# Four-layer diffusion-transformer kernel on one core: modulation rows moved between VectorE and TensorE, two convolution tiles in one PSUM bank

## The chip, the cores and the metric

The kernel runs on one core of a Trainium2 chip. The metric is the device time of one execution in microseconds (us), lower is better. The core's engines are named as in the profile: PE is TensorE's matmul and PEld its weight load, DVE is VectorE, ACT is ScalarE, POOL is GpSimd, SP is SyncE, which here issues nearly all DMAs.

## The reference, cut to what matters

The model has four layers of width 2048 over 256 tokens, with 256 context tokens that the kernel carries through layers 0 and 1. Layers 0 and 3 mix with a Fourier transform, layer 1 with window attention, layer 2 with a depthwise convolution (31 taps, one weight per channel and tap) followed by a layer norm. Each layer is modulated: a row vector of 3 x 2048 numbers (shift, scale, gate) comes from `silu(c) @ ada_w[i]`.

```python
def ada_modulation(cond, w, b):
    m = jax.nn.silu(cond) @ w + b
    return jnp.split(m, 3, axis=-1)
...
def conformer_conv_mix(h, w_in, dw_w, dw_b, ln_g, ln_b, w_out):
    a, a_gate, z = jnp.split(h @ w_in, 3, axis=-1)
    g = a * jax.nn.sigmoid(a_gate)
    ...
    y = jax.nn.silu(layer_norm(y, ln_g, ln_b))
    return (y * jax.nn.silu(z)) @ w_out
...
        shift, scale, gate = ada_modulation(c, ada_w[i], ada_b[i])
        h = rms_norm(x, norm_g[i]) * (1.0 + scale[:, None, :]) + shift[:, None, :]
        ...
        x = x + gate[:, None, :] * o
```

All inputs are float32. The kernel keeps float32 accuracy by splitting each operand in a high and a low part and adding up three products (two for the output projections).

## The kernel before, in words

**Weight pieces.** A weight matrix is streamed in pieces of 128 partitions x 1024 columns (`w_piece`, L143). Each piece has a DMA into `raw` (issued by SP, L153 or L155), a CAST on ACT to `whi` (L179), a subtraction `wlo = raw - whi` in two halves on VectorE or in one on GpSimd (L180), and its matmuls: `gemm_T` (L193 to L195) and `gemm_N` (L213 to L215) for the input projections, L1114 and L1115 for the output projections. There are three raw buffers and, up to out_proj(1), two of whi and wlo, from layer 2 on three of each (`wB`, L1181): there a piece takes the buffers of the third piece before it.

**Stages from layer 1 on.** Attention's z columns (`accz`, 32 pieces, L1075); the output projection of layer 1, written out_proj(1) below (`out_proj`, L1093, 32 pieces, accumulators `acco`); layer 2's a and gate columns in eight column groups of eight pieces (`accg`, L1217), each followed by two channel tiles `kt` of the convolution; layer 2's z columns in four groups (`accz`, L1296) with the layer norm fed in between (`ln_part`, L1260); out_proj(2); layer 3; its out_proj(3). An output projection adds to the residual on VectorE (L1126), sums squares (L416), and its last two column groups also prepare the next layer's input (L482).

**Modulation steps.** A group is one third of a layer's modulation and takes 16 steps; a step is 128 rows of ada_w times one entry of silu(c) per partition. Its 128 x 2048 block comes by two DMAs of 512 KB each into two of the four `aw` buffers (L326). On VectorE a step is two multiply-adds of 128 x 1024 into `adacc` (L279 for the first of a group, L281 else), called halves below; on TensorE it is four matmuls of 512 columns (L268), the first step of a TensorE chain with a stationary operand padded to 32 columns (`cpad`, L264). At a group's end VectorE's sums are added over partitions by four matmuls (L295), and the result goes to `modc`. The stream `ada_v` has seven groups, for (layer, third) = (1,2), (2,0) to (2,2), (3,0) to (3,2).

**The plan.** `Stream.plan(quarters, steps)` (L350) sets a goal of 4 x quarters steps in all and spreads what is missing over the coming calls of `step`, one behind each weight piece. The goals are the constants T1 to T3S: T1 in attention (56 calls), T1O in out_proj(1) (SV1 = 28 calls), T2 in accg from group 2 on, on TensorE (46 calls), T2Z in z, T2O in out_proj(2) (SV2 = 22 calls), then `nxt3` (until group (3,1) is done, T3S), then plan(28, 60) in layer 3. `ada_v.behind` (L283, L540) keeps the first half of a stage behind the start of a layer.

**The convolution.** GpSimd writes the gated tile into `gp` (L1241), ACT the first tap into PSUM with the bias (L1244), VectorE the 30 others in place (L1250), ACT copies the result out to `cv` (L1252), and the channel sums go to `csum` (GpSimd, the last on VectorE, L1258). The tile `pv` has the size of a PSUM bank and only its first half is used; there are two such buffers (tag "cv"). The taps' weights come by two DMAs (`dwr`, L1174) in `nxt2`, called at the start of out_proj(1)'s seventh column group; TensorE turns them (L1201) in layer 2.

**The order.** The Tile scheduler orders each engine's instructions statically by dependencies, buffers and priorities, so the plan's numbers and the buffers decide what stands where; an engine executes its row in order.

Of the kernel before, what the change touches and what calls it, by code (L numbers as in the profile page):

```python
# [19 lines left out]
P = 128  # L20
# [3 lines left out]
TAPS = 31  # L24
# [4 lines left out]
T0O = 9  # L29
T1 = 14.25  # L30
T1O = 18.25
T2 = 21
T2Z = 21
T2O = 24
T3S = 24.5
SA = 22
# [35 lines left out]
def dit_kernel(ctx: ExitStack, tc: tile.TileContext, x, c, ctxt, c_ctx, norm_g, ada_w, ada_b,  # L72
# [32 lines left out]
    nc.vector.memset(eps_t[:], EPS)  # L105
    sel = cp.tile([P, 2], F32, name="sel")
    for o in range(2):
        nc.vector.tensor_reduce(sel[:, o:o + 1], ident[:, o:o + 97:32], axis=AX.X, op=ALU.add)

    sel8 = cp.tile([P, 8], F32, name="sel8")  # L110
# [141 lines left out]
    def ada_group(l, s, st):  # L252
# [3 lines left out]
        for kt in range(KT):  # L256
            aw = st.get(l, s, kt)
            if st.pe:
# [4 lines left out]
                if fp:  # L263
                    cs = wp.tile([P, 40], F32, tag="cpad", name="cpad")[:, :32]  # L264
                    nc.vector.memset(cs, 0.0)
                    nc.vector.tensor_copy(cs[:, 0:2], csil[:, kt, :])
# [200 lines left out]
    class Deferred:  # L467
# [3 lines left out]
        def __init__(self, l):  # L471
            self.l, self.rs, self.done = l, None, 0
            t = wp.tile([P, 40], F32, tag="cpad", name=nm("sh"))
            self.sh, self.col = t[:, 0:2 * KT].rearrange("p (k r) -> p k r", r=2), t[:, 32:36]
            sv = modc[l][:, 0:16, 0]
            nc.scalar.copy(self.sh[:, :, 0].bitcast(F32R), sv)
            nc.vector.tensor_sub(self.sh[:, :, 1], sv, self.sh[:, :, 0])
# [40 lines left out]
        def leave(self, dst, bank, func, i):  # L518

            col = self.col[:, i:i + 1]  # L520
            nc.scalar.copy(col, bank[:, 256:257])
# [145 lines left out]
    csil0 = aw0.tile([P, 4, 32], F32, name="csil0")  # L667
    nc.gpsimd.memset(csil0[:], 0.0)
    psD = pool(l0, "psD0", PSUM)
    psa_box[0] = pool(l0, "psada0", PSUM)  # L670
# [500 lines left out]
    def nxt2():  # L1171
        for i in range(2):
            t = wp.tile([P, D // 2], F32, tag="aw", bufs=AWB, name=nm("dwr"))
            nc.sync.dma_start(t[:TAPS, :], conv_dw_w[0, :, i * 1024:(i + 1) * 1024])  # L1174
            dwr.append(t)
        return Deferred(2)
# [40 lines left out]
    for cg in range(8):  # L1217
# [20 lines left out]
        for ci in range(2):  # L1238
            kt = 2 * cg + ci
            gt = gp[kt % 4]  # L1240
            nc.gpsimd.tensor_mul(gt[:, PAD:PAD + 256], sa[:, 256 * ci:256 * ci + 256], sg[:, 256 * ci:256 * ci + 256])  # L1241
            pv = psD.tile([P, 512], F32, tag="cv", bufs=2, name=nm("pv"))
            if T0A:
                nc.scalar.activation(pv[:, :256], gt[:, 0:256], AF.Identity, bias=colT[:, kt:kt + 1],  # L1244
                                     scale=dwT[:, kt, 0:1])
            else:
                nc.vector.tensor_scalar(pv[:, :256], gt[:, 0:256], dwT[:, kt, 0:1], colT[:, kt:kt + 1],
                                    op0=ALU.mult, op1=ALU.add)
            for t in range(1, TAPS):
                nc.vector.scalar_tensor_tensor(pv[:, :256], gt[:, t:t + 256], dwT[:, kt, t:t + 1], pv[:, :256],  # L1250
                                               op0=ALU.mult, op1=ALU.add)
            nc.scalar.copy(cv[kt][:], pv[:, :256])  # L1252
            if kt == 0:
                nc.vector.tensor_copy(csum[:], pv[:, :256])
            elif CSP > kt:
                nc.gpsimd.tensor_add(csum[:], cv[kt][:], csum[:])
            else:
                nc.vector.tensor_add(csum[:], pv[:, :256], csum[:])  # L1258

# [64 lines left out]
    yh = [hp.tile([P, 2, 256], F32R, tag=f"yh{k}", name=f"yh3_{k}") for k in range(KT)]  # L1324
    ada_v.plan(28, 60)
    rbox[0] = wk
# [16 lines left out]
    for cg in range(4):  # L1343
        def piece_z(kt):
            return w_piece(w_rows(wi, kt, D + cg * 512), deint=True)

        if cg:
# [111 lines left out]
```

## Time and profile before

| | us |
|---|---|
| median of 3 runs | 1924.52 (1924.08 to 1924.67) |
| the profiled execution's own time | 1923.44 |
| its span | 1921.4 |
| TensorE busy in the span | 1859.0 |
| VectorE busy | 1452.4 |
| ScalarE busy | 911.0 |
| GpSimd busy | 224.5 |

The profile is of one execution; 1923.44 us is its device time, 1921.4 us the span from the first to the last recorded instruction. Instructions are grouped by source line; "busy" is the time in which at least one of a group ran, "mean" the duration of one, "idle before" the time its engine waited just ahead of them, with what ended the wait. A row of the windows view gives, for a stretch from A to B in us, its length, then busy time and instruction count of PE, PEld, DVE, ACT and POOL, then the granted TensorE clock, the busy share of the 16 DMA engines and the GB/s moved. By the chain of starts on PE the stages run as follows: attention's z from 966.6, out_proj(1) from 1093.0 to 1194.4, accg to 1394.9, z to 1494.5, out_proj(2) from 1494.6 to 1598.9, then layer 3. TensorE matmuls leave two records each in the counts.

### The profile page before, as it was taken

Reading aid. Unit: us, or ns where it says so; the run is one execution under the profiler, and the core shown is the slowest. Engines: PE = TensorE matmul, PEld = TensorE weight load, DVE = VectorE, ACT = ScalarE, POOL = GpSimd, SP = SyncE. Lnnn points to the kernel's source line nnn. Section 1 sums busy time; section 2 is a strip of 40 time slices with the busy share of each in tenths; the row PEclk is TensorE's granted clock in tenths of the full one; section 3 lists DMA queues with packets and bytes.
Section 4 is the critical chain, followed back from the end, with each engine's and each line's share of the span. In section 5 each row is a group of like instructions: output and inputs, shape, how many; then the busy total and the mean of one; then the engine's idle time right before and its main releaser. Section 6 shows DMA issues by size and latency. Waiting matters only on the chain.

```text
span 1921.4 us, 30258 instructions
## 1 busy us (share of the span) xinstructions
PE 1859.0 (97%) x11143; PEld 1497.9 (78%) x11143; DVE 1452.4 (76%) x2774; ACT 911.0 (47%) x1685; POOL 224.5 (12%) x124
## 2 busy tenths in 40 slices
PE   6999999999999999999999989999999899999997
PEld 5566657777776687866689978999999788889886
DVE  4899954556653458987898678688898999997675
ACT  6333342233322225455556545644455657656553
POOL 0000000000000000000000000788893000000000
PEclk9999999999999999999999999999999999999999
DMA  8888867666778754741568677577766697785553
GB/s 262 282 292 298 302 241 262 201 233 214 240 240 266 272 192 145 245 161 56 187 197 258 206 246 250 187 247 247 256 211 196 213 308 238 244 284 177 165 175 132
DMA packets 247173, 433.64 MB, mean 226 GB/s; under 512 B 16212, under 2 KB 135732, under 8 KB 247026
## 3 DMA queue, kind: packets, MB, share of 16 engines
q1 hardware_dynamic: 245728, 430.25, 68.3%
q8 instruction: 87, 1.43, 0.3%
q10 hardware_dynamic: 1298, 1.48, 0.3%
q14 instruction: 60, 0.49, 0.1%
HBM read 429.56 MB, written 2.10 MB: 225 GB/s over the span
## 4 chain that ended last, share of the span: by engine, by line
PE 78%; DVE 8%; DMA 7%; ACT 3%; issue 2%; POOL 2%; SPq 0%; ACTq 0%; DVEq 0%; POOLq 0%
PE acco L1114 7%; PE accz L193 5%; PE accz L194 5%; PE accz L195 5%; PE accu L213 4%; PE accu L214 4%; PE accu L215 4%; PE acco L1115 3%; DVE wlo L180 3%; PE pa L268 3%; PE acco L193 3%; PE acco L194 3%; PE acco L195 3%; PE accg L193 3%; PE accg L195 3%; PE accg L194 3%
## 5 line engine op out<-in xcount | busy, mean ns | idle before, releaser
L179 ACT CAST whi<-raw 128x512 fp32r<-128x512 f32 (+1 forms) x765 | 540.9, 761 | 664.0 <-PE accu L215 121.3
L180 DVE TENSOR_TENSOR wlo<-raw,whi 128x512 fp32r<-128x512 f32 x682 | 497.3, 778 | 214.7 <-ACT whi L179 209.4
L281 DVE SCALAR_TENSOR_TENSOR adacc<-aw,csil,adacc 128x1024 f32<-128x1024 f32 x188 | 242.7, 1297 | 74.8 <-DMA aw<-in_ada_w_dram 74.7
L1114 PE MATMUL acco<-yh,whi 128*128 128x512 f32 x768 | 276.1, 403 | 9.5 <-ACT whi L179 4.8
L195 PE MATMUL accz<-hx,wlo 128*128 128x256 f32 (+1 forms) x768 | 220.0, 287 | 6.8 <-DVE wlo L180 5.6
L1115 PE MATMUL acco<-yh,wlo 128*128 128x256 f32 x768 | 217.2, 285 | 2.8 <-DVE wlo L180 2.8
L193 PE MATMUL accz<-hx,whi 128*128 128x256 f32 (+1 forms) x768 | 218.0, 284 | 0.0
L194 PE MATMUL accz<-hx,whi 128*128 128x256 f32 x768 | 217.9, 284 | 0.0
L1250 DVE SCALAR_TENSOR_TENSOR pv<-gp,dwT,pv 128x256 f32<-128x256 f32 x480 | 193.0, 485 | 18.9 <-ACT pv L1244 18.3
L180 POOL TENSOR_TENSOR wlo<-raw,whi 128x1024 fp32r<-128x1024 f32 x83 | 201.7, 2441 | 40.3 <-ACT whi L179 37.6
L1114 PEld LDWEIGHTS acco<-yh,whi 128*128 128x128 f32 x768 | 146.1, 191 | 46.6 <-ACT whi L179 5.4
L195 PEld LDWEIGHTS accz<-hx,wlo 128*128 128x128 f32 x768 | 146.7, 191 | 10.3 <-DVE wlo L180 7.3
L1115 PEld LDWEIGHTS acco<-yh,wlo 128*128 128x128 f32 x768 | 146.9, 192 | 7.0 <-DVE wlo L180 5.7
L194 PEld LDWEIGHTS accz<-hx,whi 128*128 128x128 f32 x768 | 146.6, 191 | 1.2 <-issue 0.8
L193 PEld LDWEIGHTS accz<-hx,whi 128*128 128x128 f32 x768 | 146.9, 191 | 0.6 <-ACT whi L179 0.2
L193 PE MATMUL accg<-hx,whi 128*128 128x256 f32 (+1 forms) x512 | 144.9, 284 | 0.3 <-ACT hx L455 0.3
L195 PE MATMUL accg<-hx,wlo 128*128 128x256 f32 (+1 forms) x512 | 143.9, 282 | 0.0
L194 PE MATMUL accg<-hx,whi 128*128 128x256 f32 x512 | 143.3, 280 | 0.0
L1193 POOL MEMSET gp<- 128x286 f32 x4 | 1.2, 338 | 1193.3 <-PE acco L1115 1193.3
L193 PE MATMUL acco<-yh,whi 128*128 128x512 f32 (+1 forms) x272 | 105.9, 390 | 0.0
L193 PEld LDWEIGHTS accg<-hx,whi 128*128 128x128 f32 x512 | 96.2, 188 | 10.8 <-issue 10.3
L194 PE MATMUL acco<-yl,whi 128*128 128x512 f32 (+1 forms) x272 | 103.6, 381 | 0.0
(283 smaller groups left out, 3713.2 us busy)
## 6 DMA issues: line engine op xcount, KB each, us to landing
aw<-in_ada_w_dram SPq DMA_DIRECT2D x376, 512.0 KB, 5.3
raw<-in_four_w_in_dram SPq DMA_DIRECT2D x126, 512.0 KB, 4.9
raw<-in_attn_w_in_dram SPq DMA_DIRECT2D x72, 512.0 KB, 4.0
raw<-in_conv_w_in_dram SPq DMA_DIRECT2D x128, 256.0 KB, 3.4
raw<-in_four_w_out_dram SPq DMA_DIRECT2D x32, 512.0 KB, 5.8
raw<-in_attn_w_out_dram SPq DMA_DIRECT2D x64, 256.0 KB, 4.7
raw<-in_conv_w_in_dram SPq DMA_DIRECT2D x32, 512.0 KB, 4.3
raw<-in_conv_w_out_dram SPq DMA_DIRECT2D x64, 256.0 KB, 4.2
```

The source lines that it names most:

```text
L179: nc.scalar.copy(hv[:, c], iv[:, c])
L180: eng.tensor_sub(lv[:, c], iv[:, c], hv[:, c].bitcast(F32))
L193: mm(o, a, hh, start=st, stop=False, skip_group_check=True)
L194: mm(o[:, :narrow] if narrow else o, a, hl, start=False, stop=False, skip_group_check=True)
L195: mm(o, b, hh, start=False, stop=kt + k == span[1] - 1, skip_group_check=True)
L213: mm(acc[:], hh, whi[:, k, :], start=st, stop=False)
L214: mm(acc[:], hh, wlo[:, k, :], start=False, stop=False)
L215: mm(acc[:], hl, whi[:, k, :], start=False, stop=kt + k == KT - 1)
L281: ins = nc.vector.scalar_tensor_tensor(acc[:, cs], aw[i][:], cc, acc[:, cs], op0=ALU.mult, op1=ALU.add)
L1114: mm(o[:], whi[:, k, cs], rhs(kt), start=kt == 0, stop=False, skip_group_check=True)
L1115: mm(o[:, :256], wlo[:, k, cs], rhs(kt)[:, :256], start=False, stop=kt == KT - 1, skip_group_check=True)
L1250: nc.vector.scalar_tensor_tensor(pv[:, :256], gt[:, t:t + 256], dwT[:, kt, t:t + 1], pv[:, :256], op0=ALU.mult, op1=ALU.add)
```

## The change

What it does, part by part:

- **Goals of the plan.** T1 57 to 65 steps, T1O 73 to 86, T2 and T2Z 84 to 91, T3S 98 to 96 (in steps; the constants are quarters of a group's step count). So 13 steps more lie in out_proj(1) on VectorE, and accg has 5 steps on TensorE in place of 11. In layer 3 the plan is set only from the second column group on, as 46 calls, with `behind` set.
- **PSUM.** The two channel tiles of a column group share one PSUM bank, one half each (`pvb`); there are two banks still, so four tiles' room in place of two.
- **Taps.** The two `dwr` DMAs are issued by GpSimd instead of SP.
- **Small tiles.** `cpad` and `sh` shrink from 40 to 32 columns (128 bytes per partition); the four bias columns of `leave` get a tile of their own; `sel` moves to the pool of layer 0's start.

```diff
-T1 = 14.25
-T1O = 18.25
-T2 = 21
-T2Z = 21
+T1 = 16.25
+T1O = 21.5
+T2 = 22.75
+T2Z = 22.75
 T2O = 24
-T3S = 24.5
+T3S = 24
...
-                    cs = wp.tile([P, 40], F32, tag="cpad", name="cpad")[:, :32]
+                    cs = wp.tile([P, 32], F32, tag="cpad", name="cpad")[:]
...
-            t = wp.tile([P, 40], F32, tag="cpad", name=nm("sh"))
-            self.sh, self.col = t[:, 0:2 * KT].rearrange("p (k r) -> p k r", r=2), t[:, 32:36]
+            t = wp.tile([P, 32], F32, tag="cpad", name=nm("sh"))
+            self.sh = t[:].rearrange("p (k r) -> p k r", r=2)
...
+            if i == 0:
+                self.col = wp.tile([P, 4], F32, tag="rcol", bufs=2, name=nm("col"))
...
-            nc.sync.dma_start(t[:TAPS, :], conv_dw_w[0, :, i * 1024:(i + 1) * 1024])
+            nc.gpsimd.dma_start(t[:TAPS, :], conv_dw_w[0, :, i * 1024:(i + 1) * 1024])
...
-            pv = psD.tile([P, 512], F32, tag="cv", bufs=2, name=nm("pv"))
+            if ci == 0:
+                pvb = psD.tile([P, 512], F32, tag="cv", bufs=2, name=nm("pv"))
+            pv = pvb[:, 256 * ci:256 * ci + 256]
...
-    ada_v.plan(28, 60)
...
+        if cg == 1:
+            ada_v.behind = built[0]
+            ada_v.plan(28, 46)
```

In the changed kernel the lines lie up to six lines off: L277 there is L281 here (modulation half), L176 is L180 (wlo), L412 is L416, L1127 is L1126, L1253 is L1250 (tap), L1261 is L1258 (csum), L1267 is L1264 (pmean), L291 is L295, L431 and L387 are L435 and L391, L1115 and L1116 are L1114 and L1115.

The first place is VectorE's row in out_proj(1), from the second square sum of the first residual tiles on. `wlo` is a weight piece's low part, `adacc<-aw` a modulation half, `ss` a square sum, `xT` a residual tile. Before:

```order
L281 SCALAR_TENSOR_TENSOR adacc_10412<-aw_10634,csil,adacc_10412 128x1024
L180 TENSOR_TENSOR wlo_10251<-raw_10247,whi_10250 128x512 x2
L416 TENSOR_TENSOR ss_9942<-ss_9942,tmp_10181 128x256
L281 SCALAR_TENSOR_TENSOR adacc_10412<-aw_10663,csil,adacc_10412 128x1024
L180 TENSOR_TENSOR wlo_10282<-raw_10278,whi_10281 128x512 x2
L416 TENSOR_TENSOR ss_9942<-ss_9942,tmp_10186 128x256
L281 SCALAR_TENSOR_TENSOR adacc_10412<-aw_10665,csil,adacc_10412 128x1024
L180 TENSOR_TENSOR wlo_10319<-raw_10315,whi_10318 128x512 x2
L1126 SCALAR_TENSOR_TENSOR xT_90<-acco_10189,modc_83,xT_90 128x256
```

In the changed kernel, at the same place:

```order
L277 SCALAR_TENSOR_TENSOR adacc_9980<-aw_10246,csil,adacc_9980 128x1024
L277 SCALAR_TENSOR_TENSOR adacc_9980<-aw_10248,csil,adacc_9980 128x1024
L412 TENSOR_TENSOR ss_10003<-ss_10003,tmp_10254 128x256
L277 SCALAR_TENSOR_TENSOR adacc_9980<-aw_10314,csil,adacc_9980 128x1024
L176 TENSOR_TENSOR wlo_10324<-raw_10320,whi_10323 128x512 x2
L412 TENSOR_TENSOR ss_10003<-ss_10003,tmp_10259 128x256
L277 SCALAR_TENSOR_TENSOR adacc_9980<-aw_10316,csil,adacc_9980 128x1024
L277 SCALAR_TENSOR_TENSOR adacc_9980<-aw_10345,csil,adacc_9980 128x1024
L277 SCALAR_TENSOR_TENSOR adacc_9980<-aw_10347,csil,adacc_9980 128x1024
L176 TENSOR_TENSOR wlo_10355<-raw_10351,whi_10354 128x512 x2
L277 SCALAR_TENSOR_TENSOR adacc_9980<-aw_10376,csil,adacc_9980 128x1024
L277 SCALAR_TENSOR_TENSOR adacc_9980<-aw_10378,csil,adacc_9980 128x1024
```

Ahead of the next residual add stand eight modulation halves for two pieces, where there were three for three. Counted over the 32 pieces of out_proj(1) there are 44 halves in place of 18.

The second place is TensorE's row at the layer norm's start. `pmean` is the mean over channels, for which `csum` must be complete; `accz` are z's matmuls, `acco` those of out_proj(2), `pss` and `prs` the layer norm's variance and factor. Before:

```order
L193 MATMUL accz_14416<-hx_11001,whi_14694 128x256
L194 MATMUL accz_14416<-hx_11001,whi_14694 128x256
L1264 MATMUL pmean<-csum,ones 128x256
L195 MATMUL accz_14416<-hx_11001,wlo_14695 128x256
L193 MATMUL accz_14416<-hx_11010,whi_14694 128x256
L194 MATMUL accz_14416<-hx_11010,whi_14694 128x256
L195 MATMUL accz_14416<-hx_11010,wlo_14695 128x256
```

Between this L1264 and the first `acco` matmul stand 196 `accz` matmuls before. In the changed kernel the end of z and the start of out_proj(2) read:

```order
L190 MATMUL accz_14750<-hx_11101,whi_14997 128x256
L191 MATMUL accz_14750<-hx_11101,wlo_14998 128x256
L291 MATMUL pa_12299<-adacc_10720,ones 32x512 x4
L1267 MATMUL pmean<-csum,ones 128x256
L431 MATMUL pss_14477<-ones,ss_14276 128x1 x2
L431 MATMUL pss_14477<-ones,tmp_14511 128x1 x2
L387 MATMUL prs_14521<-tmp_14518,ones 128x256
L1115 MATMUL acco_15052<-yh_0_13888,whi_15057 128x512
```

All of z now stands ahead of `pmean`, and between `pmean` and the first `acco` matmul only the layer norm's own matmuls are left.

The third place is VectorE's row at the last channel tile's last taps and the channel sum. Before:

```order
L1250 SCALAR_TENSOR_TENSOR pv_13833<-gp_11035,dwT,pv_13833 128x256
L180 TENSOR_TENSOR wlo_14733<-raw_14730,whi_14732 128x512
L1250 SCALAR_TENSOR_TENSOR pv_13833<-gp_11035,dwT,pv_13833 128x256
L180 TENSOR_TENSOR wlo_14775<-raw_14772,whi_14774 128x512
L1258 TENSOR_TENSOR csum<-pv_13833,csum 128x256
L180 TENSOR_TENSOR wlo_14775<-raw_14772,whi_14774 128x512
L281 SCALAR_TENSOR_TENSOR adacc_15089<-aw_15200,csil,adacc_15089 128x1024
```

There `wlo_14775` is the second piece of z's last column group. In the changed kernel:

```order
L1253 SCALAR_TENSOR_TENSOR pv_13820<-gp_11126,dwT,pv_13820 128x256
L176 TENSOR_TENSOR wlo_15085<-raw_15081,whi_15084 128x512
L1253 SCALAR_TENSOR_TENSOR pv_13820<-gp_11126,dwT,pv_13820 128x256
L176 TENSOR_TENSOR wlo_15110<-raw_15106,whi_15109 128x512
L1261 TENSOR_TENSOR csum<-pv_13820,csum 128x256
L176 TENSOR_TENSOR wlo_15110<-raw_15106,whi_15109 128x512
L275 TENSOR_SCALAR adacc_16764<-aw_16762,csil 128x1024
```

`wlo_15085` and `wlo_15110` are the second and third piece of out_proj(2): the channel sum has moved behind all of z's pieces. The counts of the same row say where other halves went: between the start of accg and the start of out_proj(2) there are 10 in place of 5, in out_proj(2) itself at most 3 in place of 20, in layer 3 as many as before (29), but none in its first column group, which had 6.

More of the change, by code (lines that the diff above doesn't have):

```diff
@@ L105, in dit_kernel @@
     nc.vector.memset(eps_t[:], EPS)
-    sel = cp.tile([P, 2], F32, name="sel")
-    for o in range(2):
-        nc.vector.tensor_reduce(sel[:, o:o + 1], ident[:, o:o + 97:32], axis=AX.X, op=ALU.add)
     sel8 = cp.tile([P, 8], F32, name="sel8")
@@ L668, in dit_kernel @@
     nc.gpsimd.memset(csil0[:], 0.0)
+    sel = aw0.tile([P, 2], F32, name="sel")
+    for o in range(2):
+        nc.vector.tensor_reduce(sel[:, o:o + 1], ident[:, o:o + 97:32], axis=AX.X, op=ALU.add)
     psD = pool(l0, "psD0", PSUM)
@@ L1241, in dit_kernel @@
             nc.gpsimd.tensor_mul(gt[:, PAD:PAD + 256], sa[:, 256 * ci:256 * ci + 256], sg[:, 256 * ci:256 * ci + 256])
-            pv = psD.tile([P, 512], F32, tag="cv", bufs=2, name=nm("pv"))
+            if ci == 0:
+                pvb = psD.tile([P, 512], F32, tag="cv", bufs=2, name=nm("pv"))
+            pv = pvb[:, 256 * ci:256 * ci + 256]
             if T0A:
-                nc.scalar.activation(pv[:, :256], gt[:, 0:256], AF.Identity, bias=colT[:, kt:kt + 1],
+                nc.scalar.activation(pv, gt[:, 0:256], AF.Identity, bias=colT[:, kt:kt + 1],
                                      scale=dwT[:, kt, 0:1])
             else:
-                nc.vector.tensor_scalar(pv[:, :256], gt[:, 0:256], dwT[:, kt, 0:1], colT[:, kt:kt + 1],
+                nc.vector.tensor_scalar(pv, gt[:, 0:256], dwT[:, kt, 0:1], colT[:, kt:kt + 1],
                                     op0=ALU.mult, op1=ALU.add)
             for t in range(1, TAPS):
-                nc.vector.scalar_tensor_tensor(pv[:, :256], gt[:, t:t + 256], dwT[:, kt, t:t + 1], pv[:, :256],
+                nc.vector.scalar_tensor_tensor(pv, gt[:, t:t + 256], dwT[:, kt, t:t + 1], pv,
                                                op0=ALU.mult, op1=ALU.add)
-            nc.scalar.copy(cv[kt][:], pv[:, :256])
+            nc.scalar.copy(cv[kt][:], pv)
             if kt == 0:
-                nc.vector.tensor_copy(csum[:], pv[:, :256])
+                nc.vector.tensor_copy(csum[:], pv)
             elif CSP > kt:
@@ L1257, in dit_kernel @@
             else:
-                nc.vector.tensor_add(csum[:], pv[:, :256], csum[:])
+                nc.vector.tensor_add(csum[:], pv, csum[:])
     def ln_part():
```

## The prediction

> **What bounds the kernel now.** I read the page first, its busy times and its costliest groups.
>
> ```profile
> PE 1859.0 (97%) x11143; PEld 1497.9 (78%) x11143; DVE 1452.4 (76%) x2774; ACT 911.0 (47%) x1685; POOL 224.5 (12%) x124
> ...
> L281 DVE SCALAR_TENSOR_TENSOR adacc<-aw,csil,adacc 128x1024 f32<-128x1024 f32 x188 | 242.7, 1297 | 74.8 <-DMA aw<-in_ada_w_dram 74.7
> ...
> L1250 DVE SCALAR_TENSOR_TENSOR pv<-gp,dwT,pv 128x256 f32<-128x256 f32 x480 | 193.0, 485 | 18.9 <-ACT pv L1244 18.3
> ```
>
> TensorE is busy 97% of the span, so over the whole kernel it is the bound, and moving work from TensorE to VectorE (76%) looks free. That is an average over stages. The windows view, cut where the stages change, says what each stage has to give:
>
> ```profile
> 966.00:1093.00 127.00, 126.97 (x1004) 114.94 (x1002) 99.46 (x190) 74.58 (x159) 0.00 (x0) 1.00 0.69 217
> 1093.00:1194.00 101.00, 95.12 (x522) 80.82 (x519) 84.76 (x143) 48.93 (x98) 0.00 (x0) 0.97 0.77 250
> 1194.00:1395.00 201.00, 200.45 (x1671) 187.75 (x1670) 164.57 (x407) 97.69 (x137) 164.90 (x89) 1.00 0.72 235
> 1395.00:1494.00 99.00, 94.75 (x776) 93.46 (x776) 91.13 (x206) 55.45 (x99) 58.72 (x29) 0.98 0.65 207
> 1494.00:1599.00 105.00, 97.68 (x535) 81.67 (x534) 97.15 (x179) 62.10 (x127) 0.00 (x0) 0.97 0.77 253
> ```
>
> Attention's z columns (first row) are TensorE-bound and leave VectorE 27.5 us idle. In out_proj(1) (second row) VectorE has only 101 - 84.8 = 16.2 us left, and the DMA engines 23%. The a and gate columns, accg (third row), are TensorE-bound with 36 us of VectorE to spare. The z columns leave VectorE 8 us, out_proj(2) 8 us: there VectorE already sets the pace in part, and TensorE idles 7 of 105 us. So a half step added in the second row is dear, one taken from the fifth is a gain, and one taken from TensorE in the third is worth its own time.
>
> **The change part by part: out_proj(1).** The groups of VectorE in that stretch, and the halves that VectorE runs in three stretches (the same view for line L281 alone):
>
> ```profile
> L180 DVE TENSOR_TENSOR wlo<-raw,whi 128x512 fp32r<-128x512 f32 x66 | 42.4, 686 | 11.1 <-ACT whi L179 10.8
> L281 DVE SCALAR_TENSOR_TENSOR adacc<-aw,csil,adacc 128x1024 f32<-128x1024 f32 x16 | 20.5, 1280 | 2.6 <-DMA aw<-in_ada_w_dram 2.6
> ```
> ```profile
> 966.00:1093.00 127.00, 25.39 (x20) 1.00 0.69 217
> 1093.00:1194.00 101.00, 20.48 (x16) 0.97 0.77 250
> ...
> 1494.00:1599.00 105.00, 21.71 (x17) 0.97 0.77 253
> ```
>
> The order puts 44 halves between the weight pieces of out_proj(1) where 18 stood, 26 more. At 1.28 us each that is 33.3 us, and VectorE's work in the stage grows from 84.8 to 118 us. VectorE alone then needs 118 us for a stage of 101: +17, if it never waits. The low end is +12: up to 5 us of its first work may be done while attention's z still runs, since VectorE has slack there and is at most two or three pieces ahead. Attention itself I cost at nothing: up to the start of out_proj(1) both orders have the same 128 halves, and TensorE's 127 of 127 us cover them; without that cover the ten or so halves that stand later inside it would be 13 us.
>
> The DMAs give the high end. Each half fetches 512 KB (0.524 MB). The stage moved 250 GB/s x 101 us = 25.3 MB and gets 26 x 0.524 = 13.6 MB more, 38.9 MB. The best rate that I find kept up over 25 us stands in the same stage:
>
> ```profile
> 1145.00:1170.00 25.00, 25.00 (x146) 21.80 (x145) 22.67 (x40) 12.90 (x26) 0.00 (x0) 0.99 0.91 292
> ```
>
> At 292 GB/s, 38.9 MB take 133 us: +32. Between +12 and +32 I take +22, nearer to VectorE's floor of 17, since the best rate had 9% of the engines' time left; at 292 / 0.91 = 321 GB/s the transfers would need 121 us, 3 more than VectorE.
>
> **The taps' DMAs.** SP issued them in this stage; the chain of waits has, just behind, the longest transfer of the stage, and the waits view has what TensorE lost by it:
>
> ```profile
> 1127.09 12.24 DMA raw<-in_attn_w_out_dram
> ```
> ```profile
> PE acco L1114 <- ACT whi L179: 4.8, 2, 3.6
> ```
> ```profile
> dwr<-in_conv_dw_w_dram SPq DMA_DIRECT2D x2, 124.0 KB
> ```
>
> A weight piece took 12.24 us to land, and TensorE lost 4.8 us. GpSimd has nothing to do in the stage (0.00 in its row), so issuing there costs nothing, and if the transfers no longer hold SP's queue, up to 4.8 us come back. The Trainium skill ("DMA: Bandwidth & Descriptors", section "Why a DMA increments its semaphore by 16 and not by 1") has a DMA use the largest number of engines up to 16 that divides its outer dimension: 31 rows would sit on one engine. Its section "Queues, rings and completion order" lets an engine alternate between queues, by which the weight pieces would pass. The stage's rows agree with a queue that stands (12.24 us for 256 KB); none shows the other queue. I credit nothing, because VectorE's 118 us are counted without waits: with VectorE the bound, the stall was idle time that the new halves fill.
>
> **Layer 2.** accg loses six steps on TensorE and one group's end:
>
> ```profile
> L268 PE MATMUL pa<-aw,csil 128*2 128x512 f32 x72 | 9.4, 592 | 0.0
> L268 PE MATMUL pa<-aw,cpad 128*32 128x512 f32 x16 | 2.1, 604 | 0.0
> ...
> L295 PE MATMUL pa<-adacc,ones 128*32 128x512 f32 x8 | 1.1, 605 | 0.0
> ```
>
> The 88 records are 11 steps, 11.5 / 11 = 1.05 us a step; six are 6.3 us, L295 is 1.1: -7.4, call it -8 with the small matmuls behind L295. All of it counts, since TensorE has no gap there. The shared bank must not eat it: both taps chains must still fit VectorE's 36 us of slack (a rival, below).
>
> The layer norm is the other side. Before, these are the channel sum and the first matmul of out_proj(2) (first start, last start), and what VectorE did in between:
>
> ```profile
> L1258 DVE TENSOR_TENSOR csum<-pv,csum x1: 426/426/426, 1464.1 to 1464.1; 128x256 f32<-128x256 f32 x1
> ```
> ```profile
> L1114 PE MATMUL acco<-yh,whi x9: 388/397/403, 1494.6 to 1499.9; 128*128 128x512 f32 x9
> ```
> ```profile
> L180 DVE TENSOR_TENSOR wlo<-raw,whi 128x512 fp32r<-128x512 f32 x13 | 8.8, 686 | 0.0
> ...
> L281 DVE SCALAR_TENSOR_TENSOR adacc<-aw,csil,adacc 128x1024 f32<-128x1024 f32 x3 | 3.8, 1276 | 0.0
> ```
>
> 30.5 us lie between them, and TensorE filled them with 196 matmuls of z. In the changed order all of z stands ahead of `pmean`, and the channel sum behind the second piece of out_proj(2). The third piece's buffer is free only when z's last piece is used up, so TensorE idles through the layer norm. The chain is shorter by 12 of the 13 low parts that stood in it (8.2 us) and by half a microsecond of halves: 30.5 - 8.7 = 22 us of idle time (18 if all the halves' work leaves too, 28 if the three halves that stand in it wait for their DMA). Against that, z becomes shorter: its 768 matmuls start every 94.75 / 776 = 0.122 us, 94 us, less what covered the layer norm's own: -5 (3 to 6) from 99.5 us. And out_proj(2) loses at least 17 halves, 21.7 us of VectorE's 97; TensorE then sets its pace, at the 95.1 us of busy time of out_proj(1) (second row) or a little less: -10 (-8 to -12). Layer 2 together: -8 + 22 - 5 - 10 = -1 (-6 to +10).
>
> **Layer 3 and the rest.** The number of halves is the same, 29, but the six in the first column group leave it:
>
> ```profile
> 1599.00:1631.00 32.00, 28.89 (x209) 28.44 (x208) 29.88 (x46) 22.49 (x38) 0.00 (x0) 0.89 0.80 255
> 1700.00:1755.00 55.00, 53.27 (x337) 47.38 (x336) 46.59 (x66) 33.03 (x49) 0.00 (x0) 1.00 0.70 225
> ```
>
> There TensorE idles 3 us beside a VectorE that is full; the halves go to a stretch where VectorE has 8 us: -2 (-4 to +2). The small tiles, `sel` and the columns of `leave` only change where things lie: nothing, their instructions are as many as before; the cover is that all of them stand at stage ends with one answer, and a wait there would be under 1 us.
>
> **Sum.** +22 - 1 - 2 = +19. On the profiled execution, 1923.44, that is 1942.4; the median of the runs is 1.1 above that, so 1943.5, say 1943 us.
>
> **The rivals.** *TensorE stays the bound in out_proj(1).* VectorE's order is static, but its 16.2 idle us and TensorE's lost 4.8 go first; if the new halves cost the stage nothing and the 4.8 us come back, the total is 1924.5 - 5 - 1 - 2 = 1916.5, and 1910 with layer 2 at its low end (-6) and layer 3 at -4. It decides this way if out_proj(1) takes no longer than its 101 us, which needs the new halves to overlap with the stage before; 33.3 us against 16.2 speak against it. Chance 0.15.
>
> *The transfers bound out_proj(1) and the layer norm costs its high end.* +32 + 10 - 2 = +40 at most, 1951 to 1964. For it: L281 waited 74.8 us for its DMAs over the kernel. Against: 321 GB/s by the share. Chance 0.15.
>
> *The shared bank makes the taps serial.* The records of ACT on that tile:
>
> ```profile
> L1244 ACT ACTIVATE pv<-gp,colT,dwT x16: 562/569/581, 1225.6 to 1434.9; 128x256 f32<-128x256 f32 x16
> L1252 ACT COPY cv<-pv x16: 358/366/378, 1253.5 to 1463.7; 128x256 f32<-128x256 f32 x16
> ```
>
> If ACT may not touch one half while VectorE works on the other, two chains can't alternate. The group L1250 is busy 193.0 us for 480 taps, 0.402 us each, while one lasts 0.485: a chain alone costs 0.083 us more a tap, 40 us over both stretches, and each of 16 tiles adds its first tap and its copy on ACT to the chain (0.57 + 0.37 us), 15 us. Of these 55 us 36 + 8 are covered by VectorE's slack in accg and z: 11 us more, 1954. The Trainium skill speaks for it ("PSUM — Partial Sum Buffer", section "PSUM bank collisions raise a hardware error"): two engines in the same bank and partitions collide even at other columns, so the guard has to go by bank. By that rule ACT must wait for VectorE; the order agrees as far as ACT's first tap of the odd tile stands behind the copy of the even one. But the odd tile alternates with the next group's even one in the other bank, and the chains of before, in banks of their own, can't show the price. Chance 0.10.
>
> *The cost is repaid.* Out_proj(1) at its low end, +12, and layer 2 at -6, layer 3 at -4: +2, 1926, no change. Chance 0.07.
>
> **How the numbers follow.** The forecast, 1930 to 1950, gets 0.53. 0.2% of the time, 3.8 us, is about what a measurement of this kernel can tell from no change. Slower: 0.53 + 0.15 + 0.10 = 0.78. Same: 0.07. Faster: 0.15. The range leaves out the lower half of the first rival and the upper half of the second, and reaches from 1920 to 1957.
>
> **What would show it.** Right: out_proj(1), from its first `acco` matmul to accg's first, takes 113 to 133 us with VectorE busy over 95% of it; accg about 192; TensorE idle 18 to 28 us ahead of out_proj(2)'s first matmul; out_proj(2) 92 to 97. Wrong: out_proj(1) under 105 us; VectorE idle in it for DMAs at more than 10 us (the second rival); taps that start over 0.48 us apart through accg (the third); `acco` matmuls close behind z's last.

## The result, and the profile after

The changed kernel takes 1948.43 us (median of 4 runs, 1946.42 to 1951.0) against 1924.6 us: a ratio of 1.0121 with a 95% interval of 1.0105 to 1.0137. It is slower, by 23.8 us; 1943 was forecast, with 1920 to 1957 as the range. The profiled execution took 1950.32 us, 26.9 more than before's; its span is 1948.5. The stages below are read from these two executions, so they add up to 26.7 us and not to 23.8.

The page first, its busy times and the two groups that were shown of before (in this kernel L277 is the modulation half, L1253 the tap):

```profile
PE 1858.1 (95%) x11095; PEld 1498.0 (77%) x11095; DVE 1470.7 (75%) x2784; ACT 914.2 (47%) x1685; POOL 227.6 (12%) x126
...
L277 DVE SCALAR_TENSOR_TENSOR adacc<-aw,csil,adacc 128x1024 f32<-128x1024 f32 x200 | 259.0, 1305 | 85.2 <-DMA aw<-in_ada_w_dram 84.5
...
L1253 DVE SCALAR_TENSOR_TENSOR pv<-gp,dwT,pv 128x256 f32<-128x256 f32 x480 | 196.2, 479 | 19.7 <-ACT pv L1247 16.3
```

TensorE was busy for as long as before (1858 us) in a longer span: the loss is idle time. The windows view, cut at the new stage borders, in the order attention's z, out_proj(1), accg, z with the layer norm, out_proj(2):

```profile
966.00:1099.00 133.00, 130.49 (x1012) 117.15 (x1011) 113.55 (x202) 77.11 (x164) 0.00 (x0) 1.00 0.77 259
1099.00:1221.00 122.00, 102.58 (x547) 81.86 (x547) 113.73 (x171) 49.08 (x96) 1.21 (x2) 0.97 0.92 316
1221.00:1411.00 190.00, 189.42 (x1590) 184.10 (x1589) 160.15 (x386) 97.32 (x136) 164.00 (x87) 1.00 0.66 214
1411.00:1531.00 120.00, 96.57 (x792) 93.92 (x792) 106.55 (x233) 60.52 (x109) 61.59 (x31) 0.91 0.64 208
1531.00:1625.00 94.00, 94.00 (x523) 81.51 (x523) 75.32 (x155) 58.97 (x118) 0.00 (x0) 0.97 0.52 166
```

Out_proj(1) takes 122 us where it took 101, with VectorE at 93% and the DMA engines at 92%, both above TensorE's 84%. Accg has lost 10.9 us and is TensorE-bound still. Z and the layer norm together take 119.5 us where they took 99.7, and TensorE is busy in 97 of them. Out_proj(2) has lost 10.4 us and TensorE does not idle in it. By the starts of the stages' first matmuls on PE (the last row up to the end of TensorE's last record), after against before, in us:

| stage | before | after | difference | forecast |
|---|---|---|---|---|
| up to attention's first `po` matmul | 836.9 | 838.6 | +1.7 | 0 |
| attention to its last `po`, and its z | 256.1 | 260.8 | +4.7 | 0 |
| out_proj(1) | 101.4 | 122.1 | +20.7 | +22 |
| accg | 200.5 | 189.6 | -10.9 | -8 |
| z with the layer norm | 99.7 | 119.5 | +19.8 | +17 |
| out_proj(2) | 104.4 | 94.1 | -10.4 | -10 |
| layer 3 with its out_proj | 312.9 | 314.0 | +1.1 | -2 |

The first row is not shown to be the change's: the kernel before and the five runs built from it, equal up to there, reach the first `po` matmul between 834.7 and 842.2 us.

In out_proj(1) these are VectorE's groups, then what TensorE waited for (line, what ended the wait, us in total, times, longest):

```profile
L277 DVE SCALAR_TENSOR_TENSOR adacc<-aw,csil,adacc 128x1024 f32<-128x1024 f32 x40 | 50.1, 1279 | 0.7 <-DMA aw<-in_ada_w_dram 0.5
L176 DVE TENSOR_TENSOR wlo<-raw,whi 128x512 fp32r<-128x512 f32 x64 | 41.2, 685 | 4.6 <-ACT whi L175 4.4
```
```profile
PE acco L1115 <- ACT whi L175: 9.8, 7, 3.8
PE acco L1116 <- DVE wlo L176: 9.2, 9, 1.7
```

40 of the 44 halves are of this line; they take 50.1 us where 16 took 20.5. The other four are the first of a group (L275, 0.75 us each). VectorE waits 0.7 us ahead of these 40 halves, so the modulation's DMAs hold it up little: it is nearly full, and TensorE waits 19 us. Half of that is for VectorE's low parts. The other half is for casts on ACT, which itself waits for late weight transfers; SP issues many of these late, because VectorE has not yet used up the buffer (in this stretch SP waits 16.7 us for low parts and 29.8 us for halves).

At the layer norm, what TensorE waited for, the channel sum, and what VectorE waited for from 1500 to 1531 us:

```profile
PE pss L431 <- DVE ss L412: 16.6, 1, 16.6
PE acco L1115 <- DVE yh L546: 3.8, 1, 3.8
```
```profile
L1261 DVE TENSOR_TENSOR csum<-pv,csum x1: 417/417/417, 1505.0 to 1505.0; 128x256 f32<-128x256 f32 x1
```
```profile
DVE ss L412 <- ACT psq L408: 2.3, 5, 0.5
DVE rcol L382 <- ACT rcol L381: 2.3, 1, 2.3
DVE cv L1282 <- PE prs L387: 1.4, 1, 1.4
DVE adacc L277 <- DMA aw<-in_ada_w_dram: 0.9, 1, 0.9
```

Z's last matmul starts at 1503.5 and out_proj(2)'s first at 1530.67, so 25.7 us lie between the channel sum and that matmul, and TensorE has next to nothing to do in them. Of the modulation halves that stand in VectorE's row inside the layer norm one waits 0.9 us for its DMA; the case that the forecast named for its high end, all of them waiting, did not come. VectorE mostly waits for ACT (squares, the factor `rcol`) and for a small matmul on TensorE.

The idle time costs a little more than itself: the granted clock is still 0.50 from 1530 to 1534 us and 0.79 from there to 1540, when TensorE works again on out_proj(2), some 3 us of its work.

### The profile page after: what moved, and what is told of

The parts are those of the page before. It is cut to its first block, busy times and chain, and to the rows that moved or that the text cites. A ratio compares the mean times of both kernels' runs of the same rounds, so it can differ in the third digit from the quotient of the medians.

```text
span 1948.5 us, 30168 instructions
## 1 busy us (share of the span) xinstructions
PE 1858.1 (95%) x11095; PEld 1498.0 (77%) x11095; DVE 1470.7 (75%) x2784; ACT 914.2 (47%) x1685; POOL 227.6 (12%) x126
## 4 chain that ended last, share of the span: by engine, by line
PE 76%; DVE 10%; DMA 6%; ACT 3%; issue 3%; POOL 1%; SPq 1%; DVEq 0%; ACTq 0%; POOLq 0%
PE acco L1115 7%; PE accz L189 6%; PE accz L190 6%; PE accz L191 6%; PE accu L209 4%; PE accu L210 4%; PE accu L211 4%; DMA aw<-in_ada_w_dram 4%; DVE wlo L176 4%; PE acco L1116 4%; PE accg L189 3%; PE accg L191 3%; PE accg L190 3%; PE acco L189 3%; PE acco L190 3%; PE acco L191 3%
## 5 line engine op out<-in xcount | busy, mean ns | idle before, releaser
L176 DVE TENSOR_TENSOR wlo<-raw,whi 128x512 fp32r<-128x512 f32 x682 | 498.3, 776 | 200.8 <-ACT whi L175 196.4
L277 DVE SCALAR_TENSOR_TENSOR adacc<-aw,csil,adacc 128x1024 f32<-128x1024 f32 x200 | 259.0, 1305 | 85.2 <-DMA aw<-in_ada_w_dram 84.5
L1115 PE MATMUL acco<-yh,whi 128*128 128x512 f32 x768 | 276.3, 406 | 13.6 <-ACT whi L175 9.8
L1116 PE MATMUL acco<-yh,wlo 128*128 128x256 f32 x768 | 214.3, 286 | 9.4 <-DVE wlo L176 9.2
L1253 DVE SCALAR_TENSOR_TENSOR pv<-gp,dwT,pv 128x256 f32<-128x256 f32 x480 | 196.2, 479 | 19.7 <-ACT pv L1247 16.3
L176 POOL TENSOR_TENSOR wlo<-raw,whi 128x1024 fp32r<-128x1024 f32 x83 | 201.1, 2433 | 29.1 <-ACT whi L175 25.2
L1115 PEld LDWEIGHTS acco<-yh,whi 128*128 128x128 f32 x768 | 144.5, 191 | 50.0 <-ACT whi L175 12.9
L1116 PEld LDWEIGHTS acco<-yh,wlo 128*128 128x128 f32 x768 | 146.7, 193 | 17.8 <-DVE wlo L176 15.8
L191 PE MATMUL acco<-yh,wlo 128*128 128x512 f32 (+1 forms) x272 | 103.4, 380 | 0.0
```

What stands on the lines that cost most here:

```text
L176: eng.tensor_sub(lv[:, c], iv[:, c], hv[:, c].bitcast(F32))
L191: mm(o, b, hh, start=False, stop=kt + k == span[1] - 1, skip_group_check=True)
L277: ins = nc.vector.scalar_tensor_tensor(acc[:, cs], aw[i][:], cc, acc[:, cs], op0=ALU.mult, op1=ALU.add)
L1115: mm(o[:], whi[:, k, cs], rhs(kt), start=kt == 0, stop=False, skip_group_check=True)
L1116: mm(o[:, :256], wlo[:, k, cs], rhs(kt)[:, :256], start=False, stop=kt == KT - 1, skip_group_check=True)
L1253: nc.vector.scalar_tensor_tensor(pv, gt[:, t:t + 256], dwT[:, kt, t:t + 1], pv, op0=ALU.mult, op1=ALU.add)
```

## The experiments

My theory was that the change has two losses that don't depend on each other, the goals of the plan in out_proj(1) and the shared bank at the layer norm, and one part that might help, the taps' queue. The first four runs take these three apart; the small tiles have no run of their own.

**The goals alone (b_plan).** The kernel before, with the new constants and layer 3's plan:

```diff
-T1 = 14.25
-T1O = 18.25
-T2 = 21
-T2Z = 21
+T1 = 16.25
+T1O = 21.5
+T2 = 22.75
+T2Z = 22.75
...
-T3S = 24.5
+T3S = 24
...
-    ada_v.plan(28, 60)
...
+        if cg == 1:
+            ada_v.behind = built[0]
+            ada_v.plan(28, 46)
```

> The kernel before with the changed goals of the plan alone (and layer 3's plan from its second column group on); banks, taps' queue and small tiles as before. My theory is that the change has two losses that don't depend on each other: the goals fill VectorE in out_proj(1), the shared bank uncovers the layer norm. By it this run has out_proj(1) at 120 to 125 us, accg at 190, out_proj(2) at 95, TensorE idle under 8 us at the layer norm (123 z matmuls still stand behind pmean in the order) and about 1935 us (1931 to 1939). Rival: the layer norm's idle time comes from the goals too, because VectorE arrives late with the last taps; then z takes 115 us or more and the time is 1945 or more. Second rival: the goals alone are a gain and all of the loss is the bank's: 1920 or less.

Measured: 1947.65 us, ratio 1.0124 (1.0085 to 1.0163). Out_proj(1) takes 129.3 us, longer than in the changed kernel, z with the layer norm 105.4, accg 190.5, out_proj(2) 99.8. What TensorE waited for in out_proj(1):

```profile
PE acco L1114 <- ACT whi L179: 9.2, 7, 3.2
PE pdw L1201 <- DMA dwr<-in_conv_dw_w_dram: 8.8, 2, 5.8
PE acco L1115 <- DVE wlo L180: 7.5, 8, 1.7
```

The theory holds as to the place: the goals load out_proj(1) and leave most of the layer norm covered (the first rival asked for 115 us or more in z). Its number was 12 us too low, and the middle row has 8.8 us of waiting behind it: TensorE stands before the taps' transposes (L1201), which lie inside the stage in this order, and waits for the taps' transfers. The chain of waits shows a weight transfer behind them that took even longer than the one in the kernel before:

```profile
1189.05 13.52 DMA raw<-in_attn_w_out_dram
```

The second rival, a gain, falls.

**The shared bank alone (b_shared_bank).** The kernel before with the following (the lines that use the tile then say `pv` where they said `pv[:, :256]`):

```diff
-            pv = psD.tile([P, 512], F32, tag="cv", bufs=2, name=nm("pv"))
+            if ci == 0:
+                pvb = psD.tile([P, 512], F32, tag="cv", bufs=2, name=nm("pv"))
+            pv = pvb[:, 256 * ci:256 * ci + 256]
```

> The kernel before with the two tiles in one bank alone. By my theory z takes 117 to 122 us with 16 to 24 us of TensorE idle behind its last matmul, accg stays at 200, out_proj(1) at 101, and the time is 1943 (1938 to 1950), since out_proj(2) keeps its halves. Rival: the bank makes the taps serial, so accg grows as well, by 5 us or more, and the time goes past 1950. Second rival: the bank costs nothing by itself, 1922 to 1927.

Measured: 1937.78 us, ratio 1.0077 (1.0053 to 1.0102). Its z with the layer norm, then TensorE's longest wait, then ACT's copies of the last two channel tiles out of PSUM (start, length in us):

```profile
1395.00:1523.00 128.00, 99.86 (x788) 93.74 (x787) 119.82 (x237) 57.42 (x102) 63.70 (x31) 0.89 0.72 238
```
```profile
PE pss L435 <- DVE ss L416: 19.0, 1, 19.0
```
```profile
1452.91 0.36 ACT L1254 COPY cv<-pv 128x256 f32<-128x256 f32 x1
1492.59 0.37 ACT L1254 COPY cv<-pv 128x256 f32<-128x256 f32 x1 [0.68 <-DVE pv L1252]
```

The bank by itself uncovers the layer norm: z's stage grows by 29 us, with one wait of 19.0, more than the 117 to 122 us expected for the stage. The copies say how. The first tap of a group's second tile stands behind the copy of the first one, so the last tile of all has no other chain beside it: the two copies lie 39.7 us apart here, 4.9 in the kernel before (1458.8 and 1463.7) and 29.8 in the changed one (1474.5 and 1504.3). So the last channel sum starts at 1493.1 us where it started at 1464.1.

Accg stays at 201.8 us against 200.5, and VectorE has no more to do in it (162.8 us against 164.6), so the taps did not become serial as a whole. The total came out 5 us under the expectation: out_proj(2) got shorter by 10 us and layer 3 by 5.5. Ten modulation halves (13.0 us) now stand in VectorE's row beside the idle TensorE. By the starts of the halves, z has 21 in place of 7, out_proj(2) 17 in place of 19, and layer 3 with its out_proj 15 in place of 29. That fits layer 3's gain. In out_proj(2) VectorE is busy 90.4 us where it was 97.2, and TensorE idles 0.9 us where it idled 7.3; where the other 4 us come from I can't say.

**The taps' queue alone (b_taps_pool).**

```diff
-            nc.sync.dma_start(t[:TAPS, :], conv_dw_w[0, :, i * 1024:(i + 1) * 1024])
+            nc.gpsimd.dma_start(t[:TAPS, :], conv_dw_w[0, :, i * 1024:(i + 1) * 1024])
```

> The kernel before with the two taps' DMAs issued by GpSimd alone. If the taps' transfers held SP's queue, the weight piece that took 12.24 us to land comes in about 5 us, out_proj(1) goes from 101.4 to 97 us and the time is 1919 to 1921. Rival: the piece was late because of the volume that was under way, and the queue does not matter: out_proj(1) stays at 101 and the time within 2 us of before.

Measured: 1915.67 us, ratio 0.9956 (0.9936 to 0.9976): a gain, more than was expected and nearly twice the 4.8 us that TensorE was seen to wait. Out_proj(1) goes from 101.4 to 92.4 us, so the rival, by which the piece was late because of the volume under way, falls. The stretch behind the late piece, before, and the same stretch with the taps on GpSimd:

```profile
1136.00:1150.00 14.00, 10.38 (x49) 8.52 (x48) 8.57 (x16) 5.91 (x13) 0.00 (x0) 0.76 0.62 204
```
```profile
1136.00:1150.00 14.00, 14.00 (x86) 12.43 (x85) 13.95 (x25) 7.67 (x16) 0.00 (x0) 1.00 0.89 289
```

In 14 us TensorE ran 49 records where it now runs 86. (A weight matmul leaves one record, as z's 768 matmuls do; two each hold for the modulation's.) Its idle time in them was 3.6 us; at 86 records in 14 us that explains 22 of the 37. The granted clock (the last but two column) explains the rest: behind the wait, before, and with the taps on GpSimd,

```profile
1140.00:1146.00 6.00, 5.89 (x22) 4.84 (x22) 5.16 (x9) 3.93 (x10) 0.00 (x0) 0.56 0.54 181
```
```profile
1140.00:1146.00 6.00, 6.00 (x37) 5.30 (x36) 5.99 (x13) 3.25 (x7) 0.00 (x0) 1.00 0.98 332
```

TensorE was busy for 5.89 of 6 us behind the wait and got through 22 records in place of 37, at a clock of 0.56. Of the stage's 9.0 us, 5.0 are idle time (5.9 us of gaps before, 0.9 now) and some 2.6 the slower clock (0.44 of 6 us); about 1.4 I can't assign.

**The changed kernel with a bank for each tile (a_own_banks).**

```diff
-            if ci == 0:
-                pvb = psD.tile([P, 512], F32, tag="cv", bufs=2, name=nm("pv"))
-            pv = pvb[:, 256 * ci:256 * ci + 256]
+            pv = psD.tile([P, 512], F32, tag="cv", bufs=2, name=nm("pv"))[:, 0:256]
```

> The changed kernel with a bank for each tile again (goals and taps' queue as changed). By my theory the layer norm is covered again for the most part (140 z matmuls behind pmean, 17 of 22 us): z at 100 to 105 us, out_proj(1) still at 120 to 125, time 1931 (1928 to 1935). Rival: the goals delay the last taps so that the idle time stays, 1943 to 1950.

Measured: 1937.62 us, ratio 1.0070 (1.0043 to 1.0097). TensorE's longest waits in z and the layer norm:

```profile
PE accz L191 <- DVE wlo L176: 5.9, 3, 4.5
PE acco L1115 <- DVE yh L546: 1.9, 1, 1.9
```

The wait of 16.6 us is gone, z's stage is at 107.7 us and out_proj(1) still at 121.9. The rival (the goals keep the idle time) falls; the return is smaller than I expected, and the time lies above the range of 1928 to 1935. Z waits once 4.5 us for VectorE, and out_proj(2) takes 98.2 us: three of the halves that had been done in the idle time now stand in it, and TensorE idles 3.9 us where it idled not at all.

**What bounds out_proj(1) now (a_eighth_op).** The halves of that stage multiply one eighth of their columns; the rest of those sums is left out:

```diff
-                        ins = nc.vector.scalar_tensor_tensor(acc[:, cs], aw[i][:], cc, acc[:, cs],
+                        cs = slice(w * i, w * i + (P if cut[0] else w))
+                        ins = nc.vector.scalar_tensor_tensor(acc[:, cs], aw[i][:, :cs.stop - cs.start], cc, acc[:, cs],
...
+    cut = [False]
...
+    cut[0] = True
...
     st, dfr = out_proj(1, o_rows(attn_w_out[0]), lambda kt: yh[kt // 2][:, kt % 2, :], pump1, None, nxt2)
+    cut[0] = False
```

> The changed kernel, in which the modulation halves put into the stream during out_proj(1) multiply and add only the first 128 of their 1024 columns (the rest of those sums is left out); their DMAs stay 512 KB each and the order of VectorE stays as it is. My theory is that VectorE's work sets out_proj(1): without some 1.05 us in each of about 40 halves VectorE has 77 us of work there, and the stage falls from 122 us to between 92 and 101. Rival: the transfers set it; they are unchanged, so the stage stays at 116 us or more. What lies between, 102 to 115 us, is the length that the transfers alone allow. The layer norm's idle time (about 20 us) stays in both.

Measured: 1933.33 us, ratio 1.0062 (1.0042 to 1.0081), out_proj(1) 108.9 us:

```profile
1095.00:1204.00 109.00, 98.69 (x547) 81.09 (x548) 78.56 (x171) 48.91 (x96) 1.20 (x2) 0.98 0.99 353
```

Neither theory alone. With 35 us less of VectorE's work the stage loses 13 us, so VectorE sets it; but it stops at 109 and not at 92, with the DMA engines at 99% and 353 GB/s. The goals have loaded two engines up to nearly the same point: VectorE's 113.7 us of work, and 109 us of transfers. In the 8 us between 113.7 and 122 VectorE waits: by the groups of that stage 4.6 us ahead of low parts, nearly all for casts that hang on weight transfers, 0.7 ahead of halves, and 2.8 for TensorE.

**The changed kernel with the taps on SP (a_taps_sp).**

```diff
-            nc.gpsimd.dma_start(t[:TAPS, :], conv_dw_w[0, :, i * 1024:(i + 1) * 1024])
+            nc.sync.dma_start(t[:TAPS, :], conv_dw_w[0, :, i * 1024:(i + 1) * 1024])
```

> The changed kernel with the taps' two DMAs on SP's queue, as before. If the wait behind them is lost time in this kernel too, as the run with the plan's numbers alone makes it look (out_proj(1) at 129 us against 122), out_proj(1) is 127 to 131 us and the time is 1955 (1952 to 1958). By the forecast's reasoning, VectorE has other work meanwhile and the queue does not matter: 122 us and 1948.

Measured: 1952.03 us, ratio 1.0159 (1.0142 to 1.0176) against 1.0121; out_proj(1) 129.3 us against 122.1. The new row among TensorE's waits there is the one seen with the goals alone:

```profile
PE pdw L1202 <- DMA dwr<-in_conv_dw_w_dram: 7.8, 2, 5.7
```

The queue is worth 7 us in the stage here too, though VectorE is full, and 0.38% of the time by the two ratios, each against the kernel before in its own session. The forecast's reasoning, that VectorE's work covers it, falls: it doesn't cover the transposes, before which TensorE stands with all the pieces queued behind them.

**Queue or shape (b_taps_split).** The kernel before, still on SP's queue, each transfer split by rows:

```diff
-            nc.sync.dma_start(t[:TAPS, :], conv_dw_w[0, :, i * 1024:(i + 1) * 1024])
+            for r0, r1 in ((0, 16), (16, TAPS)):
+                nc.sync.dma_start(t[r0:r1, :], conv_dw_w[0, r0:r1, i * 1024:(i + 1) * 1024])
```

> The kernel before, taps still on SP's queue, each of the two DMAs split by rows in two of 16 and 15 rows. If the stall came from one DMA engine that got a transfer of 31 rows alone (the trace shows 21 to 27 GB/s in the stretch in which the weight piece was late), the split spreads it: out_proj(1) at 92 to 95 us and the time within 3 us of the run with the taps on GpSimd, 1913 to 1919. Rival: SP's queue itself is what holds the weight pieces, whatever the transfer's shape: out_proj(1) stays at 99 to 102 us and the time at 1921 to 1926.

Measured: 1916.14 us, ratio 0.9953 (0.9934 to 0.9973), out_proj(1) 94.2 us. The DMA view in 40 slices of the 27 us around the transfers, before (the engines' busy share in tenths, then GB/s) and with the split (GB/s, then the taps' transfers):

```profile
DMA  8868999999995149757457019798960000004996
GB/s 232 259 200 305 346 419 364 372 379 325 341 319 181 59 103 311 253 178 223 162 168 246 30 30 170 261 337 288 282 231 26 23 27 24 21 24 144 363 307 225
```
```profile
GB/s 263 316 379 382 384 399 360 323 310 247 222 325 296 208 68 244 319 281 179 313 266 71 244 352 229 46 102 256 135 296 285 379 256 322 249 73 299 267 223 275
...
dwr<-in_conv_dw_w_dram SPq DMA_DIRECT2D x2, 64.0 KB, 4.7
dwr<-in_conv_dw_w_dram SPq DMA_DIRECT2D x2, 60.0 KB, 3.2
```

Before there are six slices in a row, 4 us, at 21 to 27 GB/s, with the 16 engines busy for less than a tenth. At 99% busy they moved 353 GB/s in a_eighth_op, 22 each, so by this estimate 21 to 27 is what one engine moves: most had nothing left to do while one was at work. The trace's packets agree. From 1138.4 to 1142.2 us they follow one behind the other, mostly rows of 1 KB; these are rows of the weight pieces, left over on that engine. With the split this stretch is gone, on the same queue. So it was the shape of the transfer, 31 rows on one engine, that held back the weight pieces, and not SP's queue as such. This agrees with what the Trainium skill ("DMA: Bandwidth & Descriptors", section "Why a DMA increments its semaphore by 16 and not by 1") says of the number of engines that a DMA of 31 rows gets.

The run on GpSimd's queue does not tell queue from shape, since the transfer is spread there. Of the first one's 31 rows 19 start within 0.35 us while each takes at least 0.16 us, and all are through in 1.8 us; one behind the other they would need 5. No run sends the 31 rows over one engine on a queue other than the pieces'.

**Two further distributions.** Both looked for something better than the taps' move alone. c_t1 is the changed kernel with a bank for each tile (the diff of a_own_banks) and the goals of before in attention and out_proj(1):

```diff
-T1 = 16.25
-T1O = 21.5
+T1 = 14.25
+T1O = 18.25
```

> The changed kernel with own banks and the goals T1 and T1O of before (so T2 stands 18 steps on TensorE in accg, and out_proj(2) has one half left). Attention and out_proj(1) as in the kernel before with the taps on GpSimd (out_proj(1) at 92 to 93 us); accg 7 steps x 1.05 longer, 208; out_proj(2) without its 7 us of waits, 94; layer 3 at 209. Together 1912 (1908 to 1916). Rival: the seven steps cost on TensorE what out_proj(2) gives back, 1916 or more.

Measured: 1917.31 us, ratio 0.9973 (0.9959 to 0.9987): accg 208.8 us, out_proj(1) 92.8, out_proj(2) 98.4, z 103.8. Faster than before, not faster than the taps' move alone: the rival holds.

c_t86 is the kernel before with the taps on GpSimd and two steps more on TensorE:

```diff
-T2 = 21
-T2Z = 21
+T2 = 21.5
+T2Z = 21.5
```

> The kernel before with the taps on GpSimd and two steps more on TensorE in accg (13), so four to six halves fewer in out_proj(2). accg +2, out_proj(2) -3 to -4, the rest as in the run with the taps alone: 1914 (1911 to 1917). Rival: the order shifts and nothing is gained, 1916 to 1919.

Measured: 1918.84 us, ratio 0.9980 (0.9967 to 0.9993): accg 202.9 us, z 102.3 where it was 98.9, out_proj(2) 100.9. What TensorE took over came back in out_proj(2) only in part, and z grew; the rival holds again.

So the best version known is the kernel before with the taps off the single transfer of 31 rows: on GpSimd's queue (0.9956) or split on SP's (0.9953), two intervals that can't be told apart.

## Why the prediction was right, and where it was not

**The likeliest case came.** The time lies 5 us above the forecast, and the two places named, out_proj(1) and the layer norm, carry the loss. Inside out_proj(1) two errors nearly cancelled, which was luck; 4.7 us of attention were not in the sum at all. Reading stages instead of the page's 97% and 76% was the step that decided the sign.

**Out_proj(1): the sum was right by two errors.** +22 was forecast and +20.7 measured. The goals alone cost +27.8 there, and the taps' move, which I credited with nothing, gave 7 of them back. The step that failed is "I credit nothing, because VectorE's 118 us are counted without waits". The run of the taps alone shows -9.0 in the stage, the run of the changed kernel without them -7.2. The bound of 4.8 us was too low also in its own terms, since it counted TensorE's idle time in its two waits for casts (of 5.9 us in all) and not the slower clock behind them.

**The two bounds of that stage.** VectorE's floor was 118 us by the forecast; its busy time came to 113.7, in part because two of the 26 new halves are a group's first ones of 0.75 us and two low parts fewer fall into the stage (64 against 66). It was busy for 93% of the stage, where the forecast's sign asked for over 95%. The high end, 133 us at 292 GB/s, was wrong: the stage moved 316 GB/s, and with VectorE's load taken away 353. A rate seen in 25 us in which the engines were 91% busy was no ceiling. The rival that the transfers bound the stage had the right suspect but not the price: they allow 109 us.

**Attention, costed at nothing.** It took 4.7 us more. The order puts 8 halves between the q pieces and 32 between the z pieces where there were 20 and 20; VectorE then runs 113.6 us in the z stretch. TensorE waits 2.5 us where it waited for nothing, 1.4 of them for a low part, and the small matmuls that close a group (L296, eight records, 1.0 us) fall into this stage twice where they did once; about 1.2 us I can't assign. That the goals cause it is shown: all five profiled executions with T1 at 16.25 have 196.3 us from the first to the last `po` matmul, the six with 14.25 have 194.0 to 194.1, and c_t1, the changed kernel with the goals of before here, has 256.2 us in the table's row, not 260.8. Equal counts at the end of a stage did not mean equal cost inside it.

**The layer norm.** 22 us of idle time with 18 to 28 as its bounds; 25.7 measured from the channel sum on. The step that was mis-sized is the subtraction of the low parts. VectorE's work in this chain fell by 8.8 us (27.7 to 18.8), as costed (8.7), but its idle time rose from 2.8 to 6.9: part of the low parts had filled waits for ACT and TensorE that are now left open. Z without it was 93.8 us, 6 less, as costed (-5). The shared bank alone reproduces the wait (19.0), own banks remove it (16.6 to nothing): this cause is shown. Its price is 0.77% alone and 0.51% in the changed kernel (1.0121 against 1.0070), which the intervals don't tell apart.

**Accg and out_proj(2).** -8 forecast, -10.9 measured, part of the rest because the taps' transposes, 16 records and 1.2 us in all in before's accg, now stand in out_proj(1). -10 forecast in out_proj(2), -10.4 measured. The forecast's range for layer 2 as a whole, -6 to +10, is not what its terms give: added up they give -8 to +9.

**Layer 3.** -2 forecast, -0.2 measured (and +1.3 in its out_proj). In five other executions with the same plan there layer 3 took 208.4 to 209.5 us, 2.3 to 3.5 under before, so this looks like an uncertainty of one execution more than an error of the step.

**The rivals.** Serial taps: L1253 is busy 196.2 us for 480 taps, 0.41 us each, where 0.402 was measured before and one tap lasts 0.485, so most chains still alternate, across the two banks. Only the last tile of all runs alone, which the forecast overlooked in its argument; the order that it read held that delay all the same. TensorE staying the bound in out_proj(1) was refuted by the stage itself.

What stays open: why the parts don't add up. By the ratios the goals cost 1.24%, the bank 0.77% and the taps save 0.44%, which would be 1.57% together; 1.21% was measured. The intervals of the single parts are 0.2 to 0.4% wide on either side, so the gap can't be told from noise for certain. The small tiles, costed at nothing, were not run alone either: the changed kernel with own banks has them beside the goals and the taps' move, and its 0.70% lies within noise of 1.24 - 0.44 = 0.80%.

## What to carry to other kernels

Judge a move of work by the stage that it lands in, and count there not only the receiving engine but the transfers that come with the work: here one more engine was full at nearly the same point. Work that stands between two dependent steps as cover can be lost when a shared buffer orders one step behind another; look in the instruction order for what still stands between them. A small transfer whose rows all sit on one DMA engine, as these 31 did, can cost far more than its bytes; look whether a split spreads them.

## What the runs showed of the hardware that I had not expected

In a wait of 3.6 us TensorE's granted clock was halved, and it stayed so while TensorE was back at nearly full work, so a wait of that length cost more than itself. By the windows view of the kernel before, the clock was 0.80 over 1136 to 1140 us, 0.50 over 1140 to 1144 and 0.69 over 1144 to 1146, so it was halved from about 1138.4 to 1145.2; the wait lasted from 1136.5 to 1140.1. The Trainium skill ("TensorE: Matmul & The Clock Gate", section "Part 1: The HAM clock gate (the "warmup" mystery)") has the clock halved after an idle window of about 3.4 us and restored after a busy one of the same length. The trace agrees with the halving and the return, but not with these lengths counted from the wait: the clock fell 1.9 us into it and came back 5.1 us after its end.

The DMA engines kept up 353 GB/s over 109 us at 99% busy, where the best sustained rate seen before was 308 GB/s in a slice of the page (48 us). Behind two transfers of 124 KB a transfer of 256 KB, half a weight piece, took 12.24 us to land; split into 16 and 15 rows the taps' transfers landed in 4.7 and 3.2 us, and the stretch on one engine was gone.
